# A 3x3 convolution on one core: its first pair loaded in two pieces, its first casting load and its first stores put later

## The chip, the core and the metric

The kernel runs on one core of a Trainium2 chip. The metric is the device time of one execution in microseconds, the median over several runs; lower is better. TensorE (PE) multiplies, VectorE (DVE), ScalarE (ACT) and GpSimd (POOL) do the other arithmetic, and SP, ACT and POOL issue transfers (DMA), each on a queue of its own.

## What is computed

Sixteen images of 64 channels and 64x64 points are convolved with a 3x3 kernel to 128 channels, with a border of zeros:

```python
batch, c_in, h, w, c_out = 16, 64, 64, 64, 128
x_pad = np.pad(x, ((0, 0), (0, 0), (1, 1), (1, 1)), mode='constant')
for b, co, ci, kh, kw:
    output[b, co] += weight[co, ci, kh, kw] * x_pad[b, ci, kh:kh+h, kw:kw+w]
```

Input, weights and output are float32. 16.8 MB of images go in and 33.6 MB come out.

## The kernel before

Two images make a pair `p` (`NP` = 8): their 2x64 channels fill the 128 partitions, and a matmul uses 64 rows, so the two images of a pair run side by side. A pair is computed in four blocks of `RB` = 8 row pairs. With G0, G1, G2 the three rows of the weights, two neighbouring output rows share a term:

- U = G1 * (x[2j] + x[2j+1])
- even row: U + (G2-G1) * x[2j+1] + G0 * x[2j-1]
- odd row: U + (G0-G1) * x[2j] + G2 * x[2j+2]

So each block has 30 matmuls: six for `U` from the row sums `ss`, twelve for `A` (the even rows) and twelve for `Bt` (the odd rows) from the float16 image `xs`. ScalarE copies `U` out of PSUM into `ut` (L164), and VectorE adds it to `A` and `Bt` into the float32 output tiles `ots` (L174, L177), two tiles per pair, one for each image.

Images reach the chip in two ways. Pairs 0 to 3 are loaded as float32 by SP (`x0` at L45, `xf[1]` to `xf[3]` at L49), all issued at the start after the weights `w_raw` (L42); ScalarE then casts them to `xs` (`x0` at L101; `xf` at L169, in blocks 2 and 3 of the pair before). Pairs 4 to 7 come by `load` (L67), a transfer from POOL's queue that casts on its way, so that float16 lands in `xs`. `load(4)` is issued before the loop (L98), and `load(p + 4)` for p = 1 to 3 in the loop, behind the sums of pair p + 1.

The row sums are made by VectorE for pair 0 (L100, four instructions of 512 columns, each ahead of the cast of its rows) and by POOL for the others, one pair ahead, as two instructions of 1024 columns. POOL also casts the weights to `w16` (L61) and makes the two weight differences (L96, L97).

TensorE first turns the weights (L93), then runs `spin(10)`, ten matmuls on zeros into an unused tile (L56), and then the blocks.

A pair is stored when its fourth block is done: image 0 from SP at once, image 1 from ACT through the list `held`, which is emptied behind the `ut` copies of the next block, so in the next pair. The last pair is stored in two halves, after blocks 1 and 3.

The pool `opool` has eight buffers of 2 MB; `x0`, `xf` and the output tiles share them. `xpool` has five buffers for `xs`. Instructions in `keep(...)` hold their written order on their engine. A transfer is issued by its queue in the written order, and its data follow what that queue issued before.

Of the kernel before, what the change touches and what calls it, by code (L numbers as in the profile page):

```python
# [8 lines left out]
F32 = mybir.dt.float32  # L9
F16 = mybir.dt.float16  # L10


@with_exitstack
def kernel(
    ctx: ExitStack,
    tc: tile.TileContext,
    x: bass.AP,
    weight: bass.AP,
    out: bass.AP,
):  # L20
    nc = tc.nc
    B, CI, H, W = x.shape
    CO = weight.shape[0]
    assert H == 64 and W == 64 and CI == 64 and CO == 128 and B % 2 == 0
    NP = B // 2
    RB = 8

    keep = tc.keep_in_program_order
    x_rows = x.rearrange("b c h w -> (b c) h w")
    out_rows = out.rearrange("b co h w -> b co h w")  # L30
    w_flat = weight.rearrange("co ci kh kw -> co (ci kh kw)")

    const = ctx.enter_context(tc.tile_pool(name="const", bufs=1))
    psum = ctx.enter_context(tc.tile_pool(name="psum", bufs=8, space=bass.MemoryType.PSUM))
    xpool = ctx.enter_context(tc.tile_pool(name="xpool", bufs=5))
    opool = ctx.enter_context(tc.tile_pool(name="opool", bufs=8))
    spool = ctx.enter_context(tc.tile_pool(name="spool", bufs=3))
    upool = ctx.enter_context(tc.tile_pool(name="upool", bufs=4))


    w_raw = const.tile([CO, CI * 9], F32)
    nc.sync.dma_start(w_raw, w_flat)  # L42
    x0 = opool.tile([128, H, W], F32, tag="ot", name="x0")
    cuts = [(0, 18), (18, 34), (34, 50), (50, 64)]
    nc.sync.dma_start(x0, x_rows[0:128, :, :])  # L45
    xf = {}
    for p in (1, 2, 3):
        xf[p] = opool.tile([128, H, W], F32, tag="ot", name="xf")
        nc.sync.dma_start(xf[p], x_rows[128 * p : 128 * p + 128, :, :])  # L49
    zeros = const.tile([128, 512], F16)  # L50
    keep(nc.vector.memset(zeros, 0.0))  # L51
    warm = psum.tile([128, 512], F32, tag="acc", name="warm")

    def spin(n):
        for _ in range(n):
            keep(nc.tensor.matmul(warm, zeros[:, 0:128], zeros))  # L56

    ident = const.tile([128, 128], F16)
    make_identity(nc, ident)
    w16 = const.tile([CO, CI * 9], F16)  # L60
    keep(nc.gpsimd.tensor_copy(w16, w_raw))  # L61

    xs = {p: xpool.tile([128, H, W], F16, tag="xs", name="xs") for p in range(4)}

    def load(p):
        xs[p] = xpool.tile([128, H, W], F16, tag="xs", name="xs")
        keep(nc.gpsimd.dma_start(xs[p], x_rows[128 * p : 128 * p + 128, :, :]))  # L67

    ss = {}

    def sums(eng, p, src, lo, n):
        if p not in ss:
            ss[p] = spool.tile([128, H // 2, W], F16, tag="ss", name="ss")
        v = src.rearrange("p (j i) c -> p j i c", i=2)
        keep(
            eng.tensor_add(  # L76
                ss[p][:, lo : lo + n, :], v[:, lo : lo + n, 0, :], v[:, lo : lo + n, 1, :]
            )
        )


    Wt = const.tile([128, 5, 3, CO], F16)
    G0, G21, G1, G01, G2 = range(5)

    def wrow(i):
        return Wt[:, i, :, :].rearrange("p t c -> p (t c)")

    for kh, g in ((1, G1), (2, G2), (0, G0)):
        wp = psum.tile([128, 512], F32, tag="acc", name="wp")
        for k in range(3):  # L90
            t = 3 * kh + k
            for q in (0, 64):
                keep(nc.tensor.matmul(wp[q : q + 64, k * CO : k * CO + CO], w16[:, t::9], ident))  # L93
        keep(nc.scalar.copy(wrow(g), wp[:, 0 : 3 * CO]))  # L94
    spin(10)
    keep(nc.gpsimd.tensor_sub(wrow(G21), wrow(G2), wrow(G1)))  # L96
    keep(nc.gpsimd.tensor_sub(wrow(G01), wrow(G0), wrow(G1)))  # L97
    load(4)  # L98
    for n, (lo, hi) in enumerate(cuts):
        sums(nc.vector, 0, x0, RB * n, RB)  # L100
        keep(nc.scalar.copy(xs[0][:, lo:hi, :], x0[:, lo:hi, :]))  # L101

    held = []

    def store(eng, p, b2, ot, lo, hi):
        return eng.dma_start(
            out_rows[2 * p + b2, :, lo:hi, :],
            ot.rearrange("p j i c -> p (j i) c")[:, lo:hi, :],
        )

    for p in range(NP):
        if p + 1 < NP:
            for lo in (0, 16):
                sums(nc.gpsimd, p + 1, xf.get(p + 1, xs[p + 1]), lo, 16)
        if p > 0 and p + 4 < NP:
            load(p + 4)
        ots = [
            opool.tile([128, H // 2, 2, W], F32, tag="ot", name="ot") for _ in range(2)
        ]
        for blk in range(4):  # L120
            j0 = blk * RB

            def group(wi_rows):

                tiles = [
                    psum.tile([128, RB, W], F32, tag="acc", name="acc") for _ in range(2)
                ]
                n = 3 * len(wi_rows)
                i = 0
                for wi, off in wi_rows:  # L130
                    for kw in (1, 0, 2):
                        c_lo, c_hi = max(0, 1 - kw), min(W, W + 1 - kw)
                        for b2 in range(2):
                            p0 = 64 * b2
                            lo, hi = j0, j0 + RB
                            if off is None:
                                rhs = ss[p][p0 : p0 + 64, lo:hi, c_lo + kw - 1 : c_hi + kw - 1]
                            else:
                                while 2 * lo + off < 0:
                                    lo += 1  # L140
                                while 2 * (hi - 1) + off > H - 1:
                                    hi -= 1
                                first = 2 * lo + off
                                last = 2 * (hi - 1) + off
                                rhs = xs[p][
                                    p0 : p0 + 64,
                                    first : last + 1 : 2,
                                    c_lo + kw - 1 : c_hi + kw - 1,
                                ]
                            nc.tensor.matmul(  # L150
                                tiles[b2][:, lo - j0 : hi - j0, c_lo:c_hi],
                                Wt[p0 : p0 + 64, wi, kw, :],
                                rhs,
                                start=i == 0,
                                stop=i == n - 1,
                            )
                        i += 1
                return tiles

            U = group([(G1, None)])  # L160
            us = []
            for b2 in range(2):
                ut = upool.tile([128, RB, W], F32, tag="ut", name="ut")
                keep(nc.scalar.copy(ut, U[b2]))  # L164
                us.append(ut)
            if p + 1 in xf:
                q = p + 1
                for lo in {2: (0, 16), 3: (32, 48)}.get(blk, ()):
                    keep(nc.scalar.copy(xs[q][:, lo : lo + 16, :], xf[q][:, lo : lo + 16, :]))  # L169
            while held:  # L170
                keep(store(nc.scalar, *held.pop(0)))
            A = group([(G21, 1), (G0, -1)])
            for b2 in range(2):
                nc.vector.tensor_add(ots[b2][:, j0 : j0 + RB, 0, :], A[b2], us[b2])  # L174
            Bt = group([(G01, 0), (G2, 2)])
            for b2 in range(2):
                nc.vector.tensor_add(ots[b2][:, j0 : j0 + RB, 1, :], Bt[b2], us[b2])  # L177
            parts = {3: (0, 64)} if p < NP - 1 else {1: (0, 32), 3: (32, 64)}
            if blk in parts:
                lo, hi = parts[blk]  # L180
                store(nc.sync, p, 0, ots[0], lo, hi)
                held.append((p, 1, ots[1], lo, hi))
    while held:
        keep(store(nc.scalar, *held.pop(0)))
# [30 lines left out]
```

## Time and profile before

| | |
|---|---|
| time before, median of 3 runs | 126.43 us (126.39 to 126.6) |
| span of the profiled execution, first to last instruction | 124.8 us |
| TensorE busy in it | 108.2 us (87%) |
| VectorE, ScalarE, GpSimd busy | 82.8, 52.0, 36.2 us |
| read from and written to memory | 17.07 and 33.55 MB |
| first real matmul, end of the last one | 9.92 us, about 112.6 us |
| last two stores issued | 113.3 and 114.0 us |
| issue to landing, `x0` | 7.6 us |
| issue to landing, `xf` (shortest, median, longest) | 14.5, 22.1, 29.1 us |
| issue to landing, stores (shortest, median, longest) | 9.9, 18.7, 25.7 us |

All times of the trace count from the first instruction of the profiled execution. Its own device time is not listed beside its span; the median of the runs is 1.6 us above the span, and that part, before the first and after the last instruction, is not in any row. The page names each group by line, engine, operation and tiles. Its GB/s count a transfer by the bytes it writes, so a casting load counts half of what it reads. q1 is SP's queue, q10 ACT's, q0 POOL's.

### The profile page before, as it was taken

The page shows a single profiled execution, that of the slowest core. Times are in us where ns is not written, and L with a number is a line of the kernel's source. Part 1 is how long each engine was busy: PE and PEld are TensorE (multiplying, and loading weights), DVE is VectorE, ACT ScalarE, POOL GpSimd, SP SyncE. Part 2 cuts the span into 40 slices and gives each one's busy share as a digit, 9 for nine tenths or more (in the row PEclk, how much of TensorE's full clock was granted, in tenths as well). Part 3 has the DMA queues.
Part 4 walks back from the last instruction along what each step waited for, and adds up shares of the span by engine and source line. Part 5 has one row for each costly group of instructions (what it writes and reads, how often), then busy time and mean ns, then how long its engine had stood idle before and what let it go on. Part 6 is the DMA issues. An engine that isn't in the chain of part 4 may idle for free.

```text
span 124.8 us, 2437 instructions
## 1 busy us (share of the span) xinstructions
PE 108.2 (87%) x988; PEld 49.3 (40%) x988; DVE 82.8 (66%) x133; ACT 52.0 (42%) x84; POOL 36.2 (29%) x27
## 2 busy tenths in 40 slices
PE   0699999999999999999999999999999999990000
PEld 0433444444444444444444444444444444440000
DVE  0016787878878787877777778777877787685000
ACT  4319749833993399333333333333333333330000
POOL 2360086294799202920067000940000000000000
PEclk9999999999999999999999999999999999999555
DMA  6899999999999999999999999999999999999991
GB/s 173 362 436 407 297 323 349 425 315 415 397 349 368 305 376 373 360 334 362 381 347 360 334 344 412 431 431 425 425 441 420 436 415 425 436 412 418 436 402 74
DMA packets 3898, 46.57 MB, mean 373 GB/s; under 512 B 432, under 2 KB 432, under 8 KB 560
## 3 DMA queue, kind: packets, MB, share of 16 engines
q1 hardware_dynamic: 2016, 25.46, 49.5%
q10 hardware_dynamic: 1296, 16.78, 31.6%
q0 software_dynamic: 576, 4.19, 16.1%
q8 instruction: 7, 0.11, 0.3%
q14 instruction: 3, 0.02, 0.0%
HBM read 17.07 MB, written 33.55 MB: 406 GB/s over the span
## 4 chain that ended last, share of the span: by engine, by line
PE 86%; DMA 2%; DVE 1%; issue 1%; POOL 1%; DVEq 0%
PE acc L150 81%; PE warm L56 4%; DMA w_raw<-in_weight_dram 2%; PE wp L93 1%; DVE ot L174 1%; POOL w L61 1%; DVE ot L177 0%; DVEq L210 0%; DVEq L174 0%
## 5 line engine op out<-in xcount | busy, mean ns | idle before, releaser
L150 PE MATMUL acc<-xs,Wt 64*128 64x504 f16 (+3 forms) x768 | 87.0, 373 | 0.0
L150 PEld LDWEIGHTS <-Wt 64*128 64x128 f16 x960 | 46.8, 94 | 56.2 <-issue 0.8
L164 ACT COPY ut<-acc 128x512 f32<-128x512 f32 x64 | 34.3, 588 | 52.9 <-issue 32.1
L174 DVE TENSOR_TENSOR ot<-acc,ut 128x512 f32<-128x512 f32 x64 | 41.2, 686 | 22.6 <-PE acc L150 18.3
L177 DVE TENSOR_TENSOR ot<-acc,ut 128x512 f32<-128x512 f32 x64 | 41.1, 684 | 0.0
L150 PE MATMUL acc<-ss,Wt 64*128 64x504 f16 (+1 forms) x192 | 26.0, 377 | 0.0
L76 POOL TENSOR_TENSOR ss<-xs 128x1024 f16<-128x1024 f16 x8 | 16.8, 2124 | 20.2 <-DMA xs<-in_x_dram 20.2
L76 POOL TENSOR_TENSOR ss<-xf 128x1024 f16<-128x1024 f32 x6 | 14.1, 2361 | 13.6 <-DMA xf<-in_x_dram 13.6
L169 ACT CAST xs<-xf 128x1024 f16<-128x1024 f32 x12 | 12.0, 1058 | 0.0
L76 DVE TENSOR_TENSOR ss<-x 128x512 f16<-128x512 f32 x4 | 2.5, 687 | 7.7 <-DMA x<-in_x_dram 7.7
L93 PE MATMUL wp<-ident,w 128*64 128x128 f16 x18 | 1.3, 328 | 4.3 <-POOL w L61 4.3
L101 ACT CAST xs<-x 128x1024 f16<-128x1024 f32 (+2 forms) x4 | 3.9, 1042 | 2.6 <-DMA x<-in_x_dram 2.6
L67 POOL DMA_DIRECT2D xs<-in_x_dram x4 | 2.4, 600 | 7.8 <-ACT xs L169 7.8
L56 PE MATMUL warm<-zeros 128*128 128x512 f16 x10 | 4.4, 631 | 0.0
L93 PEld LDWEIGHTS <-w 128*64 128x64 f16 x18 | 1.1, 210 | 4.3 <-POOL w L61 4.3
L94 ACT CAST Wt<-wp 128x384 f16<-128x384 f32 x3 | 1.2, 487 | 2.9 <-PE wp L93 2.9
L56 PEld LDWEIGHTS <-zeros 128*128 128x128 f16 x10 | 1.3, 143 | 2.3 <-issue 2.2
L94 ACT ACT_TABLE_LOAD x1 | 1.3, 1283 | 0.7 <-PEq L199 0.7
L96 POOL TENSOR_TENSOR Wt<-Wt 128x384 f16<-128x384 f16 x1 | 0.9, 907 | 1.7 <-ACT Wt L94 1.7
L61 POOL CAST w<-w_raw 128x576 f16<-128x576 f32 x1 | 0.7, 663 | 2.3 <-DMA w_raw<-in_weight_dram 2.3
L97 POOL TENSOR_TENSOR Wt<-Wt 128x384 f16<-128x384 f16 x1 | 0.9, 910 | 0.0
L51 DVE MEMSET zeros<- 128x256 uint32 x1 | 0.3, 272 | 0.9 <-PEq L199 0.9
(6 smaller groups left out, 0.9 us busy)
## 6 DMA issues: line engine op xcount, KB each, us to landing
out_dram<-ot SPq DMA_DIRECT2D x7, 2048.0 KB, 22.0
out_dram<-ot ACTq DMA_DIRECT2D x7, 2048.0 KB, 18.9
xf<-in_x_dram SPq DMA_DIRECT2D x3, 2048.0 KB, 22.1
xs<-in_x_dram POOLq DMA_DIRECT2D x4, 1024.0 KB, 23.4
x<-in_x_dram SPq DMA_DIRECT2D x1, 2048.0 KB, 7.6
out_dram<-ot SPq DMA_DIRECT2D x2, 1024.0 KB, 10.6
out_dram<-ot ACTq DMA_DIRECT2D x2, 1024.0 KB, 11.0
w_raw<-in_weight_dram SPq DMA_DIRECT2D x1, 288.0 KB, 2.8
```

What stands on the lines that cost most here:

```text
L56: keep(nc.tensor.matmul(warm, zeros[:, 0:128], zeros))
L61: keep(nc.gpsimd.tensor_copy(w16, w_raw))
L67: keep(nc.gpsimd.dma_start(xs[p], x_rows[128 * p : 128 * p + 128, :, :]))
L76: eng.tensor_add(ss[p][:, lo : lo + n, :], v[:, lo : lo + n, 0, :], v[:, lo : lo + n, 1, :])
L93: keep(nc.tensor.matmul(wp[q : q + 64, k * CO : k * CO + CO], w16[:, t::9], ident))
L94: keep(nc.scalar.copy(wrow(g), wp[:, 0 : 3 * CO]))
L101: keep(nc.scalar.copy(xs[0][:, lo:hi, :], x0[:, lo:hi, :]))
L150: nc.tensor.matmul(tiles[b2][:, lo - j0 : hi - j0, c_lo:c_hi], Wt[p0 : p0 + 64, wi, kw, :], rhs, start=i == 0, stop=i == n - 1,)
L164: keep(nc.scalar.copy(ut, U[b2]))
L169: keep(nc.scalar.copy(xs[q][:, lo : lo + 16, :], xf[q][:, lo : lo + 16, :]))
L174: nc.vector.tensor_add(ots[b2][:, j0 : j0 + RB, 0, :], A[b2], us[b2])
L177: nc.vector.tensor_add(ots[b2][:, j0 : j0 + RB, 1, :], Bt[b2], us[b2])
```

## The change

Four things are changed at the start of the kernel; the arithmetic stays as it is.

1. `x0` is loaded in two transfers, rows 0 to 17 and rows 18 to 63. In place of ten spins behind the turning of the weights there are six ahead of it and two behind it.
2. VectorE makes the sums of the first two blocks of pair 0 and POOL those of the other two in one instruction; a copy of one column into `hold` orders POOL's behind VectorE's. The casts of `x0` are spread: the first ahead of the loop, the others behind the `ut` copies of blocks 0 to 2 of pair 0.
3. `load(4)` is no longer ahead of the loop but in it, at p = 0, behind POOL's sums of pair 1.
4. The two stores of pair 0 wait. At the beginning of pair 1 POOL copies the last element of `xf[3]` into `hold32`, and then copies one column of each output tile of pair 0 onto itself; the stores, which read those tiles, come after that. SP's store is written there, and ACT's goes through `held` in block 1 of pair 1. The sums of pair 2 and `load(5)` stand behind these copies on POOL.

The additions of VectorE into the output tiles also hold their written order now.

```diff
-    nc.sync.dma_start(x0, x_rows[0:128, :, :])
+    for lo, hi in ((0, 18), (18, H)):
+        nc.sync.dma_start(x0[:, lo:hi, :], x_rows[0:128, lo:hi, :])
...
+    spin(6)
     for kh, g in ((1, G1), (2, G2), (0, G0)):
...
         keep(nc.scalar.copy(wrow(g), wp[:, 0 : 3 * CO]))
-    spin(10)
+    spin(2)
     keep(nc.gpsimd.tensor_sub(wrow(G21), wrow(G2), wrow(G1)))
     keep(nc.gpsimd.tensor_sub(wrow(G01), wrow(G0), wrow(G1)))
-    load(4)
-    for n, (lo, hi) in enumerate(cuts):
-        sums(nc.vector, 0, x0, RB * n, RB)
+    sums(nc.vector, 0, x0, 0, RB)
+    sums(nc.vector, 0, x0, RB, RB)
+    hold32 = const.tile([128, 1], F32)
+    hold = const.tile([128, 1], F16)
+    keep(nc.gpsimd.tensor_copy(hold, ss[0][:, 2 * RB - 1, 0:1]))
+    sums(nc.gpsimd, 0, x0, 2 * RB, 2 * RB)
+
+    def first_cast(n):
+        lo, hi = cuts[n]
         keep(nc.scalar.copy(xs[0][:, lo:hi, :], x0[:, lo:hi, :]))
 
+    first_cast(0)
+
     held = []
+    gate = []
...
     for p in range(NP):
+        if p == 1:
+            keep(nc.gpsimd.tensor_copy(hold32, xf[3][:, H - 1, W - 1 : W]))
+            for ot in gate:
+                end = ot[:, H // 2 - 1, 1, W - 1 : W]
+                keep(nc.gpsimd.tensor_copy(end, end))
+            store(nc.sync, 0, 0, gate[0], 0, H)
+            held.append((0, 1, gate[1], 0, H))
         if p + 1 < NP:
             for lo in (0, 16):
                 sums(nc.gpsimd, p + 1, xf.get(p + 1, xs[p + 1]), lo, 16)
-        if p > 0 and p + 4 < NP:
+        if p + 4 < NP:
             load(p + 4)
...
+            if p == 0 and blk < 3:
+                first_cast(blk + 1)
...
-            while held:
+            while held and (p != 1 or blk == 1):
                 keep(store(nc.scalar, *held.pop(0)))
             A = group([(G21, 1), (G0, -1)])
             for b2 in range(2):
-                nc.vector.tensor_add(ots[b2][:, j0 : j0 + RB, 0, :], A[b2], us[b2])
+                keep(nc.vector.tensor_add(ots[b2][:, j0 : j0 + RB, 0, :], A[b2], us[b2]))
...
-            if blk in parts:
+            if p == 0 and blk == 3:
+                gate = ots
+            elif blk in parts:
```

## The prediction

> **What bounds the kernel now.** I read the page's head, busy shares and chain first, then time windows. The chain names TensorE almost alone:
>
> ```profile
> span 124.8 us, 2437 instructions
> PE 108.2 (87%) x988; PEld 49.3 (40%) x988; DVE 82.8 (66%) x133; ACT 52.0 (42%) x84; POOL 36.2 (29%) x27
> PE 86%; DMA 2%; DVE 1%; issue 1%; POOL 1%; DVEq 0%
> HBM read 17.07 MB, written 33.55 MB: 406 GB/s over the span
> ```
>
> That chain is followed back from the last instruction and holds no store. TensorE ends at 112.6, the last stores are issued at 113.3 and 114.0, and the span runs to 124.8. A last store is 1.05 MB, the two need 4.9 us at 430 GB/s, yet the issue list gives them 10.6 and 11.0 us to landing. So other stores were still queued ahead of them. The windows say since when (last two columns: busy share of the DMA engines, GB/s):
>
> ```profile
> 1.50:3.00 1.50, 0.00 (x0) 0.00 (x0) 0.00 (x0) 0.52 (x1) 0.00 (x0) 1.00 1.23 348
> 3.00:4.50 1.50, 0.20 (x4) 0.20 (x4) 0.00 (x0) 0.00 (x0) 0.66 (x1) 1.00 0.72 275
> 4.50:11.50 7.00, 7.00 (x44) 3.05 (x44) 2.50 (x4) 3.94 (x6) 2.42 (x3) 1.00 1.01 431
> 11.50:21.00 9.50, 9.50 (x92) 4.32 (x90) 7.33 (x12) 6.73 (x12) 4.69 (x2) 1.00 1.03 321
> 21.00:25.00 4.00, 4.00 (x42) 1.86 (x38) 2.67 (x6) 3.50 (x6) 0.70 (x1) 1.00 0.99 422
> 25.00:28.50 3.50, 3.50 (x36) 1.57 (x34) 2.77 (x5) 1.07 (x2) 3.50 (x2) 1.00 0.98 309
> 28.50:33.00 4.50, 4.50 (x44) 2.05 (x42) 3.77 (x7) 2.96 (x4) 2.15 (x3) 1.00 1.02 430
> 33.00:78.00 45.00, 45.00 (x426) 20.61 (x424) 35.31 (x58) 20.70 (x34) 17.21 (x10) 1.00 1.02 357
> 78.00:112.00 34.00, 34.00 (x320) 15.54 (x318) 26.27 (x43) 11.81 (x22) 4.20 (x2) 1.00 1.01 429
> 112.00:121.00 9.00, 0.55 (x6) 0.10 (x2) 1.92 (x4) 0.00 (x0) 0.00 (x0) 0.70 0.99 420
> 121.00:123.50 2.50, 0.00 (x0) 0.00 (x0) 0.00 (x0) 0.00 (x0) 0.00 (x0) 0.50 0.42 174
> ```
>
> A casting load counts here by its 1.05 MB written, though it reads 2.10 MB. Add the missing 1.05 MB: 321 becomes 431 in 11.5 to 21, and three more loads lift 357 to 427 in 33 to 78. So the transfers run at about 430 GB/s from 4.5 us to the ragged end, whatever the mixture, with one hole, 25 to 28.5 us. Read and written bytes together are 50.6 MB, 117.7 us at 430; data moves from 1.7 to 123.4 us, 121.7 us. Of the 4.0 us over, the start loses 0.6 (to 4.5), the hole 1.0, the ragged end 1.4; the rest is spread thin. **The transfers are the bound, not TensorE.** TensorE's own slack: at 114.0 the queues hold work until about 123, 9 us, of which 4.9 are the last two stores; so four microseconds of lateness would cost nothing, and earliness brings nothing.
>
> **What is in the hole.** In 25 to 28.5 only SP's queue moves:
>
> ```profile
> q1 hardware_dynamic: 69, 1.08, 98.3%
> ```
>
> 1.08 MB in 3.5 us is half a transfer: the rest of the fourth pair's load `xf[3]` (issued about 2.2, slowest landing 29.1 us later). The first store goes onto the same queue behind that load just before the hole:
>
> ```profile
> 23.70 0.35 SPq L106 DMA_DIRECT2D out_dram<-ot  x1
> 24.30 0.38 ACTq L106 DMA_DIRECT2D out_dram<-ot  x1
> ```
>
> Later stores, issued behind stores or beside casting loads, leave no such hole (420 to 430 in the later windows up to 121). I read it as the price of stores put behind loads; it is inferred from the order alone.
>
> **The parts.** The profile's span is 124.8; the median of the runs, 126.43, is 1.6 longer, which I add at the end.
>
> *First pair in pieces.* SP issues one transfer more (0.42 us by its L45 row); the later loads go out 0.4 us later behind a queue that holds 5 us of data: 0. By bytes, rows 0 to 17 are 28% of `x0`'s 5.2 us (8.80 less `w_raw`'s landing at 3.5): they land near 5.2. Six of the spins (0.43 each) now run before `w16` is there, 1.2 to 3.8, and end before the weight transposes may start at 4.3; the two behind end at 6.5. DVE's first sum (0.69) is done by 6.0, ScalarE's first cast (1.15), behind the weight copies, by 7.35; so the first block runs from about 6.5 to 9.9, not 9.92 to 13.09. Block 1 needs DVE's second sum (8.85 + 0.69 = 9.5), block 2 POOL's half (one 2.35 us instruction after the tiny `hold` copy, done by 12.1, needed at 13.0). TensorE is 3.2 us earlier, and all of it falls into slack: 0. More packets for the same bytes: nothing to 0.2; I take 0.05, since the 1.05 MB stores with half-size packets still run at 420.
>
> *`load(4)` behind the sums of pair 1.* On POOL it moves past its half of pair 0's sums and past pair 1's. Before, it is issued early, and its bytes come later:
>
> ```profile
> 7.63 0.70 POOL L67 DMA_DIRECT2D xs<-in_x_dram  x1
> 16.19 4.69 POOL L76 TENSOR_TENSOR ss<-xf 128x1024 f16<-128x1024 f32 x2 [7.86 <-DMA xf<-in_x_dram]
> 11.50:12.00 0.50, 0.50 (x8) 0.21 (x6) 0.00 (x0) 0.50 (x2) 0.00 (x0) 1.00 1.16 360
> ```
>
> At 11.5 the rate falls from 426 to 360, a casting load's mark: 3.9 us after issue. Now the plain loads have the engines alone: each 2.10 MB in 4.87 us behind `x0` at 8.8, so `xf[1]` lands at 13.7, `xf[2]` at 18.5, `xf[3]` at 23.4, its last byte some 0.6 earlier. POOL's sums of pair 1 take 13.7 to 18.4, `load(4)` is issued then, its bytes begin at 22.3: just as the plain loads run out at 22.8. It is needed at pair 4, near 57 us: 0. The Trainium skill, "DMA: Bandwidth & Descriptors", section "Specifications", gives a transfer from GpSimd about 1 us to its first byte. This trace shows 3.9 under load. By the page the load would start at 19.4 and the sum be 0.3 us more; it does not go into the sum.
>
> *The gate.* At pair 1 POOL waits for `xf[3]` (23.4 plus 0.3 of wake-up), makes three one-column copies (a 128x1 POOL instruction is 0.10 in this trace) and SP issues the first store near 24.0 instead of 23.7; a SP transfer's first byte comes 1.0 after issue (`w_raw`: 0.74, data from 1.7), so 25.0. Behind the waiting copy on POOL stand pair 2's sums and `load(5)`: sums 23.9 to 28.6, before 24.3 to 29.0. ACT's store stands behind block 1's copies, about 24.5; no one waits for it. From 22.8 to 25.0 the casting load is alone on the engines, with 5 us of work begun at 22.3. No row shows it alone. Bounds: 431 as in the mixture (0), or half, its share beside one other queue (1.1). I take 0.2, nearer the mixture, whose engines were full, and for engines that end their loads unevenly. The removed hole is worth 3.5 x (430-309)/430 = 1.0, bounds 0 and 1.0.
>
> Sum: -1.0 + 0.2 + 0.05 = -0.75 on the span, 124.0; with the 1.6 outside it 125.7.
>
> **Rivals.** *The hole stays* (it belongs to the first stores, or to chance): nothing is won and the handover costs 0.2: 126.6, of itself 126.2 to 126.9. For it: a hole seen once in one execution proves no cause. Against: its start 1.3 us after the first store's issue. *The engines run dry at the gate* (the slower side): if `load(4)`'s bytes come after 22.8, as POOL's sums or its issue are late, each microsecond of lateness is one lost, up to 2.2 (22.8 to 25.0); beyond 0.8 it eats the gain. At 2.0 late the time is 126.43 - 0.75 + 2.0 = 127.7. For it: the margin is 0.5 us; `load(5)`, issued at 28.9, leaves the rate at 430 until 33, so it is no quicker. *The casting load comes early*, at 19.4: `xf[3]`'s last byte comes at 26.2, the casting load ends at 27.8, the stores' bytes begin near 28.1: 0.3 idle and 0.2 for the uneven ends; 126.0. This is the page's rule; the trace speaks against it. *TensorE sets the end after all*, as the chain has it: 3.2 us earlier, 123.2; the saturated windows speak against it.
>
> **Numbers.** Forecast 0.55 (its own range 125.1 to 126.2), hole stays 0.20, runs dry 0.16, casting load early 0.05, TensorE 0.04. The range 125.0 to 127.0 holds nearly all of the first two, the third case and the milder part of running dry. This kernel's measurement tells 0.2%, 0.25 us, from no change. Faster: 0.52 of the forecast, 0.04 and 0.04: 0.60. Same: 0.03 of the forecast, 0.12 of the hole, 0.01: 0.16. Slower: 0.08 and 0.16: 0.24.
>
> **What would show it.** Right: no window under 400 GB/s (casting loads counted double) between 4.5 and 121; TensorE's first real matmul near 6.5, its end near 109, and the last stores' landing time longer, 13 us instead of 10.6, since they queue. Wrong: a low window at 22 to 26 (dry) or after the first stores wherever they are (the hole belongs to them); or last stores that land in under 10 us.

## Result: 1.4% slower, where 0.6% faster was forecast

The changed kernel takes 128.34 us (median of 4 runs, 127.89 to 129.04) against 126.41 us before: the ratio is 1.0142, 95% interval 1.0111 to 1.0174. Runs more than 1.5% above the fastest run of their kernel are left out of the ratios in this document. The profiled execution took 127.99 us, 126.2 of it span. On the engines the edits do what was drawn, though 0.9 us later than forecast at the first block and 2.6 us later at the gate; the time went the other way.

The engines and queues of the changed kernel, from its timeline (start, duration, engine, line, operation, count):

```profile
7.38 0.83 PE L168 MATMUL acc<-ss,Wt 64*128 64x512 f16 x6 [1.26 <-DVE ss L77]
19.41 0.70 POOL L68 DMA_DIRECT2D xs<-in_x_dram  x1
26.32 0.18 POOL L124 COPY hold<-xf 128x1 f32<-128x1 f32 x1 [6.20 <-DMA xf<-in_x_dram]
26.64 7.70 SPq L117 DMA_DIRECT2D out_dram<-ot  x2
26.76 0.38 ACTq L117 DMA_DIRECT2D out_dram<-ot  x1
31.33 0.57 POOL L68 DMA_DIRECT2D xs<-in_x_dram  x1
```

TensorE starts its blocks at 7.38 instead of 9.92 us, `load(4)` goes out at 19.4, the gate opens at 26.3, the first stores follow, and `load(5)` goes out at 31.3 (28.9 before). The windows of the same execution (start and end, length, busy time of the engines, granted clock, and in the last two columns the busy share of the DMA engines and GB/s):

```profile
1.50:3.00 1.50, 1.50 (x5) 0.59 (x4) 0.00 (x0) 0.51 (x1) 0.00 (x0) 1.00 0.88 250
3.00:4.50 1.50, 1.10 (x7) 0.20 (x5) 0.00 (x0) 0.00 (x0) 0.67 (x1) 1.00 0.92 257
4.50:7.00 2.50, 1.62 (x20) 1.15 (x21) 1.02 (x1) 2.08 (x4) 1.13 (x2) 1.00 1.08 408
22.00:27.50 5.50, 5.50 (x55) 2.97 (x52) 4.42 (x8) 1.42 (x3) 1.18 (x4) 1.00 1.03 262
27.50:30.00 2.50, 2.50 (x26) 1.40 (x24) 1.77 (x4) 2.48 (x4) 2.50 (x2) 1.00 0.98 360
35.00:40.00 5.00, 5.00 (x50) 2.72 (x47) 4.08 (x7) 1.07 (x2) 4.98 (x4) 1.00 1.02 318
121.00:122.50 1.50, 0.00 (x0) 0.00 (x0) 0.00 (x0) 0.00 (x0) 0.00 (x0) 0.50 0.83 350
122.50:125.00 2.50, 0.00 (x0) 0.00 (x0) 0.00 (x0) 0.00 (x0) 0.00 (x0) 0.50 0.14 59
```

The hole at 25 to 28.5 is gone: 0.95 MB of the bytes in 22 to 27.5 are the casting load's, and counted double they lift 262 to about 430. But a new hole stands at 35 to 40, where the kernel before had 346, or some 430 with its casting load counted double. The traffic of the new hole by queue, from the view of the transfers over that window (packets, MB, share):

```profile
q10 hardware_dynamic: 51, 0.82, 49.1%
q0 software_dynamic: 36, 0.29, 28.1%
q1 hardware_dynamic: 39, 0.48, 24.6%
```

With the casting load's 0.29 MB doubled that is 1.88 MB in 5 us, 376 GB/s at a full busy share: the engines are not idle, their packets take longer. And the end is more ragged. Before, the last stretch was

```profile
121.00:122.50 1.50, 0.00 (x0) 0.00 (x0) 0.00 (x0) 0.00 (x0) 0.00 (x0) 0.50 0.62 262
122.50:125.00 2.50, 0.00 (x0) 0.00 (x0) 0.00 (x0) 0.00 (x0) 0.00 (x0) 0.50 0.04 16
```

After, 59 GB/s over 2.5 us is what two of the 16 engines would move (an estimate: 430 / 16 = 27 GB/s each): a few still work when the others are done.

The ledger, from the bytes of each queue in the trace (casting loads by what they read), in us lost against 431 GB/s from the first byte at 1.7 us to the last:

| stretch (us) | before | changed |
|---|---|---|
| to 7: weights and first pair | 0.86 | 1.44 |
| 7 to 21 | 0.12 | 0.09 |
| 21 to 30 | 1.01 | 0.13 |
| 30 to 45 | 0.13 | 0.75 |
| 45 to 121 | 0.85 | 1.13 |
| 121 to the last byte | 1.15 | 1.90 |
| last byte at | 123.35 | 124.64 |

So 0.9 is won in the old hole, and 0.6, 0.6, 0.3 and 0.75 are lost at the start, in the new hole, in the middle and at the end. Together that is 1.3 of the 1.9 us between the medians; the profiled execution was itself 0.35 us faster than the median, and no row shows the rest. Put by engine: the 16 DMA engines end on average at 122.2 before and 122.8 after (the area under the number of active engines), the last one 1.1 and 1.9 us behind that average. So 0.55 of the loss is work that takes longer on the average engine, and 0.74 is the slowest engine that falls further behind.

### The profile page after: what moved, and what is told of

Same layout as the page of the kernel before. It is cut to its first block, busy times and chain, and to the rows that moved or that the text cites. A ratio compares the mean times of both kernels' runs of the same rounds, so it can differ in the third digit from the quotient of the medians.

```text
span 126.2 us, 2439 instructions
## 1 busy us (share of the span) xinstructions
PE 107.2 (85%) x986; PEld 58.3 (46%) x986; DVE 82.2 (65%) x131; ACT 51.8 (41%) x84; POOL 39.6 (31%) x32
## 4 chain that ended last, share of the span: by engine, by line
PE 80%; DMA 4%; DVE 2%; issue 1%; DVEq 0%; SPq 0%
PE acc L168 80%; DMA x<-in_x_dram 4%; DVE ss L77 1%; DVE ot L194 1%; DVE ot L197 0%; DVEq L232 0%; SPq L42 0%; DVEq L194 0%
## 5 line engine op out<-in xcount | busy, mean ns | idle before, releaser
L168 PEld LDWEIGHTS <-Wt 64*128 64x128 f16 x960 | 56.3, 94 | 47.7 <-issue 1.4
L168 PE MATMUL acc<-ss,Wt 64*128 64x504 f16 (+1 forms) x192 | 26.6, 377 | 1.3 <-DVE ss L77 1.3
L77 DVE TENSOR_TENSOR ss<-x 128x512 f16<-128x512 f32 x2 | 2.0, 1019 | 7.4 <-DMA x<-in_x_dram 7.4
L57 PE MATMUL warm<-zeros 128*128 128x512 f16 x8 | 3.3, 568 | 1.2 <-DVE zeros L52 1.2
L77 POOL TENSOR_TENSOR ss<-x 128x1024 f16<-128x1024 f32 x1 | 2.4, 2365 | 0.0
L57 PEld LDWEIGHTS <-zeros 128*128 128x128 f16 x8 | 0.8, 127 | 2.4 <-DVE zeros L52 1.2
L98 POOL TENSOR_TENSOR Wt<-Wt 128x384 f16<-128x384 f16 x1 | 0.9, 911 | 1.6 <-ACT Wt L96 1.6
```

The costliest lines, as they stand in the source:

```text
L77: eng.tensor_add(ss[p][:, lo : lo + n, :], v[:, lo : lo + n, 0, :], v[:, lo : lo + n, 1, :])
L168: nc.tensor.matmul(tiles[b2][:, lo - j0 : hi - j0, c_lo:c_hi], Wt[p0 : p0 + 64, wi, kw, :], rhs, start=i == 0, stop=i == n - 1,)
```

## The experiments

All ratios are to the kernel before, measured beside it on the same chip. They need not equal the quotient of two medians.

| kernel | ratio | 95% interval |
|---|---|---|
| changed, second measurement | 1.0109 | 1.0041 to 1.0178 |
| changed, x0 whole | 1.0069 | 1.0036 to 1.0103 |
| changed, x0 in halves | 1.0066 | 1.0027 to 1.0104 |
| changed, six spins behind | 1.0133 | 1.0098 to 1.0168 |
| changed, load(4) early | 1.0331 | 1.0297 to 1.0365 |
| changed, load(5) ahead of the gate | 1.0049 | 1.0020 to 1.0078 |
| the same, x0 whole | 1.0060 | 1.0038 to 1.0081 |
| changed, gate open | 1.0100 | 1.0061 to 1.0138 |
| changed, no gate | 1.0016 | 0.9991 to 1.0041 |
| no gate, POOL still waits | 0.9999 | 0.9976 to 1.0023 |
| no gate, x0 whole | 1.0026 | 0.9993 to 1.0059 |
| before, x0 split | 1.0022 | 0.9998 to 1.0045 |
| before, load(4) late | 1.0008 | 0.9977 to 1.0038 |
| before, pair 0 stored from ACT | 1.0021 | 0.9988 to 1.0054 |
| before, 17 spins | 1.0031 | 0.9989 to 1.0074 |

**Which part costs.** First the parts one by one: the changed kernel with `x0` whole,

```diff
-    for lo, hi in ((0, 18), (18, H)):
-        nc.sync.dma_start(x0[:, lo:hi, :], x_rows[0:128, lo:hi, :])
+    nc.sync.dma_start(x0, x_rows[0:128, :, :])
```

> The changed kernel with one part undone: x0 is loaded in one transfer again. Theory S (the split: the 4608-byte packets of the first piece come slowly and unevenly, 0.6 us lost by 7 us into the span and one DMA engine left behind, and as every transfer is dealt out evenly to the 16 engines this one is late to the end): about 126.0, 2 us under the changed kernel, data up to 430 GB/s from 4.5 us as before. Theory G (the gate and the later casting load change the mixture of loads and stores, and that is what costs): still 128. TensorE starts some 2.5 us later than in the changed kernel in either case, which neither counts.

without the gate,

```diff
-        if p == 1:
...
-            while held and (p != 1 or blk == 1):
+            while held:
...
-            if p == 0 and blk == 3:
-                gate = ots
-            elif blk in parts:
+            if blk in parts:
```

> The changed kernel without the gate: pair 0 is stored when its fourth block is done, as before. Theory S: 128, since the split is still there, or up to 1 us more if the hole of the first stores behind the fourth pair's load comes back. Theory G: 126.5, since the gate is gone.

with `load(4)` early,

```diff
+    load(4)
     sums(nc.vector, 0, x0, 0, RB)
...
-        if p + 4 < NP:
+        if p > 0 and p + 4 < NP:
```

> The changed kernel with load(4) ahead of the loop again, on POOL behind the weight differences. Theory S: 128, split still there. Theory G, if it is the place of the casting load that costs: 126.5; the stores then wait for a fourth load that lands near 28, with the engines dry for about 2 us at the gate: up to 130 if that is not covered.

and the split alone, put into the kernel before (the first diff of this section the other way round):

> The kernel before with one thing changed: x0 is loaded in two transfers, rows 0 to 17 and 18 to 63; sums, casts, spins, loads and stores stay. Theory S: 127.5 to 128.5, 1 to 2 us slower than before. Theory G: 126.4, no difference.

Measured: 1.0069, 1.0016, 1.0331 and 1.0022. Theory S falls as the whole cause: the split alone measures 0.2%, which its interval does not tell from nothing, and without the gate nothing is left that the measurement can tell from no change. Theory G holds for the gate, not for the place of the casting load. Yet with the gate in place about half of the loss goes with the split: 1.0069 without it, against 1.0142 and 1.0109 with it (the interval of the second overlaps). In the profiles the last DMA engine ends 1.1 us behind the average with `x0` whole, as before, and 1.9 and 2.1 in the two of the changed kernel. Why the two parts together cost more than each alone stays open; in the profile with `x0` whole TensorE also ends 2.2 us later than before (114.8 us), so that ratio holds another loss as well. The start is slower with the split all the same: the kernel before with the split alone has this at the start, as the changed kernel has.

```profile
1.50:3.00 1.50, 0.00 (x0) 0.00 (x0) 0.00 (x0) 0.51 (x1) 0.00 (x0) 1.00 0.82 229
3.00:4.50 1.50, 0.10 (x2) 0.10 (x3) 0.00 (x0) 0.00 (x0) 0.66 (x1) 1.00 0.95 278
4.50:7.00 2.50, 2.50 (x22) 1.56 (x23) 0.69 (x1) 1.94 (x4) 1.00 (x1) 1.00 1.05 408
```

Before, the first of these windows moved 348, and the last

```profile
4.50:7.00 2.50, 2.50 (x22) 1.51 (x21) 0.00 (x0) 1.24 (x3) 1.09 (x2) 1.00 1.04 446
```

The three together moved 2.05 MB, here 1.78. That is 0.6 us by packets that start in the windows (0.5 us by the ledger's count), and of it some 0.3 us (0.2%) arrive in the time, no more than the interval leaves open. With `load(4)` early the engines do run dry at the gate:

```profile
25.00:28.00 3.00, 3.00 (x31) 1.64 (x28) 2.27 (x5) 1.07 (x2) 0.00 (x0) 1.00 0.92 393
28.00:30.50 2.50, 2.50 (x28) 1.35 (x24) 1.11 (x2) 0.07 (x1) 1.01 (x4) 1.00 0.05 13
```

A share of 0.05 for 2.5 us is what an empty queue looks like; the hole at 35 to 40, with a share of 1.02, is something else. This is the price of the rival "the engines run dry at the gate", reached by another road: `load(4)`'s bytes are spent before the gate opens. It is not what happens in the changed kernel, where 22 to 27.5 us has a share of 1.03.

**The mark again, the parts together, and two sizes.** The changed kernel once more:

> The changed kernel itself once more, as the mark for the three beside it. 128.0 to 128.7 if its first measurement holds. Theory E (every transfer waits for the slowest of the 16 DMA engines, and the gate makes the stores wait for that engine too): the fourth pair's load lands at 26 or later although its bytes are over by 23 on most engines, and the last second of the span moves little. Theory G2 (the gate's own wait leaves the engines without work): a window at 22 to 29 well under 430.

128.55 us, 1.0109. The landing time fits the first half of theory E: in the first profile the fourth pair's load is over on the first engine at 22.8 us and on the last at 25.9, and POOL's wait ends at 26.3; in the second the engines end between 23.0 and 26.0. The casting load has its first bytes at 22.8, so the engine that is last shares its time with it. The split is not what spreads them: with `x0` whole the two loads before it spread by 0.6 us, and this one still from 22.5 to 26.5. Whether the wait for the last engine is what costs is tested below (gate open). From 21 to 35 us this second profile loses 0.3 us in all, so theory G2 falls.

Both split and gate undone (the diffs of the first two together):

> The changed kernel with both the split and the gate undone; the late load(4), the spins ahead and the spread sums and casts stay. If split and gate are all that costs: 126.3 to 126.6, no difference from before. If the later load(4) costs by itself: 127 or more.

1.0026: no difference that can be told, as expected. But its profile, of one of its longest runs (127.85 us, the median is 127.34), shows that the late stores alone are not the whole story. TensorE started its blocks at 10.9 us there, and without any gate the first stores were issued nearly as late as behind it (26.64 and 26.76):

```profile
26.05 0.35 SPq L116 DMA_DIRECT2D out_dram<-ot  x1
26.65 0.38 ACTq L116 DMA_DIRECT2D out_dram<-ot  x1
```

Seventeen spins in the kernel before:

```diff
-    spin(10)
+    spin(17)
```

> The kernel before with 17 spins in place of 10: TensorE starts 3.0 us later, nothing else is changed. If the transfers are the bound and TensorE has some 4 us of slack: 126.4 to 126.9. If TensorE's chain sets the end, as the chain of waits has it: 129.4.

The edit did less than it was meant to: the later spins take 0.2 us each, so TensorE started only 1.15 us later (11.07 instead of 9.92). The ratio is 1.0031, not told from no change. Its profile (128.21 us) shows work missing at 100 to 107 us, where the engines that are ahead wait for pair 6 (before: 429 GB/s over 78 to 112):

```profile
100.00:107.00 7.00, 7.00 (x70) 3.25 (x68) 5.69 (x10) 2.15 (x4) 0.00 (x0) 1.00 0.95 398
```

That is 0.5 us of missing work. So TensorE is not the bound, but in that profile its slack there is under the 1.15 us by which it started later, not 4.

`x0` cut at row 34:

```diff
-    for lo, hi in ((0, 18), (18, H)):
+    for lo, hi in ((0, 34), (34, H)):
```

> The changed kernel with x0 cut at row 34 in place of row 18, so that the first piece has packets of 8704 bytes, not 4608. If the small packets are what makes the start slow: under 0.75 us lost between 2.5 and 7 us in place of 1.1, and 0.3 us or more off the time. If a second transfer as such is what costs: no difference.

1.0066 against 1.0109 beside it; the intervals overlap. The start loses 0.8 us between 2.5 and 7 us in place of 1.0 to 1.1, a little less with the larger packets, but two holes of 0.9 us each follow between 33 and 45. Inconclusive for the time.

**What the old hole was.** The prediction took it for the price of a store queued behind a load. In the kernel before, pair 0 goes to ACT's queue with both images:

```diff
+                if p == 0:
+                    held.append((p, 0, ots[0], lo, hi))
+                else:
                     store(nc.sync, p, 0, ots[0], lo, hi)
```

> The kernel before with both stores of pair 0 issued by ACT, so that no store stands behind a load on SP's queue; ACT's come at about 24.3 and 24.7 us, nothing waits longer. Theory H1 (the hole is the price of a store queued behind loads, as the prediction had it): no window under 400 GB/s between 21 and 33, 125.4 to 125.9. Theory H2 (the hole is a price of starting a transfer on a queue while the engines are full, wherever it is queued): the hole is still there or moved, 126.4 to 126.9.

The hole is still there; timeline, window and the queues in the window 25 to 28.5:

```profile
24.09 0.38 ACTq L106 DMA_DIRECT2D out_dram<-ot  x1
24.54 0.40 ACTq L106 DMA_DIRECT2D out_dram<-ot  x1
25.00:28.50 3.50, 3.50 (x36) 1.84 (x33) 2.65 (x5) 1.07 (x2) 3.50 (x2) 1.00 1.02 332
q1 hardware_dynamic: 68, 1.03, 93.1%
q10 hardware_dynamic: 8, 0.13, 8.7%
```

SP's queue holds loads alone, no store stands behind them, and its packets still crawl. H1 falls, and with it the 1.0 us that the gate was to win.

All seventeen profiles side by side say more (half microseconds under 380 GB/s, casting loads counted double). In six of them both the first stores and `load(5)` wait for `xf[3]`: there a slow stretch begins 4.1 to 4.7 us after `load(5)` is issued. In the other eleven one begins 1.4 to 3.2 us after the first store is issued, the kernel before among them. That speaks for the rival that the hole belongs to the first stores, with a second pattern beside it; it is order in time again, not a cause.

**By which way the gate costs.** The gate opened, `load(5)` put ahead of it, and the late `load(4)` alone in the kernel before:

```diff
-            keep(nc.gpsimd.tensor_copy(hold32, xf[3][:, H - 1, W - 1 : W]))
+            keep(nc.gpsimd.tensor_copy(hold32, xf[1][:, H - 1, W - 1 : W]))
```

> The changed kernel with the gate open: hold32 is copied from xf[1], which landed long before, in place of xf[3]; the copies, their places and ACT's store in block 1 stay. The stores of pair 0 are then issued near 21.5 to 24. If the wait for the slowest engine's end of the fourth pair's load is what the gate costs: 126.6 to 127.1, as without the gate. If the copies or the places cost: 128 and more.

```diff
         if p + 4 < NP:
             load(p + 4)
+        if p == 1:
...
```

> The changed kernel with the gate behind pair 2's sums and load(5) on POOL, so that load(5) is issued near 25 and not at 31.3, while the first stores still wait for xf[3]. If the delay of the casting loads behind the gate is what costs: 126.5 to 127. If the late start of the stores itself costs (the engines then have only casting loads until 28): 128 or more. The slow stretch at 35 to 40 should move ahead by 6 us if it belongs to the start of load(5).

```diff
-    load(4)
     for n, (lo, hi) in enumerate(cuts):
...
-        if p > 0 and p + 4 < NP:
+        if p + 4 < NP:
```

> The kernel before with load(4) in the loop at p = 0, behind pair 1's sums, nothing else: x0 whole, no gate, sums and spins as before. If the later casting load costs nothing, as the prediction had it: 126.3 to 126.7. If it costs by itself: over 127.

1.0100, 1.0049 and 1.0008. The late `load(4)` is free, as predicted. With `load(5)` ahead of the gate over half of the loss is gone and the slow stretch does move, to 28 to 32 us. The open gate did not help: 127.75 us in the median. So the wait for the slowest engine's end of `xf[3]` is not shown to be the price: without it 1.0% is still lost. Its profile is of its fastest run (126.63 us) and so shows nothing of its loss. In that profile the gate's copies wait for pair 0's last additions,

```profile
24.09 0.18 POOL L127 COPY ot<-ot 128x1 f32<-128x1 f32 x1 [3.72 <-DVE ot L197]
24.68 0.18 POOL L127 COPY ot<-ot 128x1 f32<-128x1 f32 x1 [0.41 <-DVE ot L197]
```

so SP's store is issued at 24.3 and ACT's at 27.3, against 20.9 and 21.5 without the gate and 23.7 and 24.3 in the kernel before.

The last three: `load(5)` held back without the stores (in the kernel without the gate, only the copy into `hold32` at p = 1), four spins more, and the stores held back with `x0` whole and `load(5)` early.

```diff
     for p in range(NP):
+        if p == 1:
+            keep(nc.gpsimd.tensor_copy(hold32, xf[3][:, H - 1, W - 1 : W]))
```

> The changed kernel with the stores of pair 0 free (as in the run without the gate), but with POOL still waiting for xf[3] ahead of pair 2's sums, so that load(5) is issued as late as in the changed kernel, near 31 us instead of 25. Theory L (the gate costs by what it holds back on POOL: the later casting loads): 127.5 to 128.5. Theory W (the gate costs by the late stores themselves): 126.6 to 127.0, as without the gate.

```diff
-    spin(2)
+    spin(6)
```

> The changed kernel with six spins and not two behind the weights, so that TensorE goes without a pause from 4.3 us into the first block and starts it near 8 us at full rate in every run. If the pause ahead of the first block (1.3 us, with its first matmuls at half rate in some runs) is part of the loss or of its spread: 127.5 or less and runs that lie closer together. If the transfers alone decide: no difference, 128 to 128.6.

> The changed kernel with load(5) ahead of the gate on POOL and x0 in one transfer: both parts undone that cost so far, the wait of the stores stays. If these two are the whole loss: 126.3 to 126.7. If the late stores cost 0.3% by themselves: 126.9 to 127.2.

0.9999, 1.0133 and 1.0060. Theory L falls: `load(5)` late, with the stores free, costs nothing. Kernels with held-back stores measure 0.5 to 0.6% more with `load(5)` early, and 0.7 to 1.4% with `load(5)` late as well. Four spins more changed nothing in the loss; the first block started at 8.4 us, not at full rate as expected, since its first six matmuls still took 1.46 us. In the last kernel the engines end evenly, but TensorE starts at 9.6 us, ends its last matmul at 114.7 (112.5 before), and the engines lack work near 105:

```profile
103.00:107.00 4.00, 4.00 (x40) 2.19 (x38) 2.77 (x5) 1.75 (x4) 0.00 (x0) 1.00 0.94 393
102.67 6.69 SPq L116 DMA_DIRECT2D out_dram<-ot  x2
```

So part of its 0.6% is another loss, in a place where the changed kernel has none.

What is settled: the loss goes when the gate goes. Each kernel with the first stores behind POOL's copies measures 0.5 to 1.4% slower (3.3% where the queues run empty), and each without them is within about 0.3% of before. What is not: by which way the gate costs. The kernel with the gate open, whose stores come 0.6 us (SP) and 3.0 us (ACT) later than before in its one profile, loses 1%, and the one without gate and split issues them almost as late as the gated ones without a loss that can be told. And it stays open why packets run slowly, at the worst at half rate, somewhere between 21 and 45 us in these profiles. No kernel here beats the one before beyond its interval.

## Why the prediction was wrong, point by point

*The transfers are the bound: right.* TensorE was 2.5 us earlier, its last matmul near 110 instead of 112.6, and none of it was won; the last stores took longer to land, as the prediction said. Before and after:

```profile
out_dram<-ot SPq DMA_DIRECT2D x2, 1024.0 KB, 10.6
out_dram<-ot SPq DMA_DIRECT2D x2, 1024.0 KB, 15.1
```

But the slack of four microseconds was read only at the end. With 17 spins work was missing already at 100 to 107 us, where the seventh pair's stores come in.

*"The removed hole is worth 1.0": this step failed.* It rested on order in time alone, and the prediction named the rival that the hole stays. The hole does not come from stores behind loads on one queue (pair 0 from ACT). Under the gate the hole at 25 to 28.5 was gone and one stood at 35 to 40, which took 0.6 of the 0.9 us back. In two gated kernels, `x0` whole and `x0` in halves, there were two such stretches between 30 and 45, about 2 us in all. The rival gave 126.2 to 126.9, and 128.34 was measured; the rest of the profile's loss is in the terms below, and why the gate brings it stays open.

*The uneven engines: missing from the sum.* The prediction added up GB/s, as if the 16 engines were one pipe, and put the landing of `xf[3]` at 23.4. The first engine was done with it at 22.8, as forecast, but the last at 25.9, and the gate opened at 26.3, since POOL's wait ended only behind the last one. That lateness is measured; that it costs is not shown, as the open gate has it. The end of the span is again the slowest engine's, 0.74 us further behind the average than before: a term that the sum did not have. The 0.2 us for the handover and the margin of 0.5 us were sound: 21 to 30 us lost 0.1, and from 25.5 to 27.5, with nothing beside it, the casting load ran at 430 to 434 GB/s (its bytes counted double), the better of the prediction's two bounds.

*The split: 0.05 was too little for the start.* The first seven microseconds lost 0.6 more than before. Alone the split measures 0.2% or 0.3 us, not told from nothing, against the 0 to 0.2 us that the prediction allowed; the first piece landed near 6.0, not 5.2, and the first sum took 1.34 us, not 0.69, beside the weight differences on POOL, so the block began at 7.4 and not 6.5.

*`load(4)`: right.* It was issued 1 us later than forecast (19.4), needed 3.4 us to its first bytes (22.8), and alone in the kernel before it costs nothing. The Trainium skill, "DMA: Bandwidth & Descriptors", section "Specifications", has about 1 us to the first byte for such a transfer; this trace disagrees again. What a casting load that starts well ahead of the end of the plain loads does at the gate is seen with `load(4)` early: the engines were dry for about 2.4 us there, not for the 0.3 us of the rival that had it come early.

*Running dry: its mechanism is real, its condition was not met.* It needed late bytes of `load(4)`; they came in time.

## What to carry to other kernels

Where the DMA engines are full from start to end, as here, an order of transfers can only win what a stretch of slow packets or an uneven engine loses: look for these, engine by engine, before pricing a reorder by mean GB/s. Price a wait on a whole transfer by the last of its engines (here 25.9 us), not by the first (22.8). And a dip in the rate that follows some issue is a guess until a kernel without that issue has been run; its busy share tells a dry queue (0.05) from slow packets (1.0).

## What was not expected of the hardware

Slow stretches at a full busy share occur in every profile here between 21 and 45 us, once or twice and of different length and depth (0.5 to 3 us under 380 GB/s), at places that a reorder moves. The slow packets are not those of one queue. In the kernel before they are SP's loads (0.89 us in the mean at 25.5 to 28.5, in place of 0.61 for 16 KB); with `load(4)` late and no gate they are the casting load's (0.90 in place of 0.62 at 25 to 28.5), while SP's take 0.62.

TensorE's first six matmuls on `ss` take 0.83 us in the first profile of the changed kernel and 1.47 in the second, both behind the same two spins of the same program:

```profile
7.57 1.47 PE L168 MATMUL acc<-ss,Wt 64*128 64x512 f16 x6 [0.82 <-DVE ss L77]
8.80 3.49 PE L168 MATMUL acc<-xs,Wt 64*128 64x512 f16 x16
```

There TensorE ended 2.7 us later; the granted clock column shows full speed in both. The Trainium skill, "TensorE: Matmul & The Clock Gate", section "Part 1: The HAM clock gate (the "warmup" mystery)", tells of half rate until a free-running window of some 3.4 us has been busy, so that the change comes at varying places; this would fit, and no run here shows the window itself.
